# A decoder step on one core: selection and one-hot rows merged into one stream, expert rows fetched ahead, final norm without GpSimd

## The chip, the cores and the metric

The kernel runs on one core of a Trainium2 chip. The metric is the device time of one launch in microseconds (us): 2086.35 is the median of three runs (2083.2 to 2087.53). TensorE (PE in the profile) multiplies, VectorE (DVE) and ScalarE (ACT) do elementwise work, GpSimd (POOL) issues indirect transfers, SyncE (SP) issues most of the other transfers. Each engine works its own instructions in order; 16 DMA engines carry the transfers.

## What is computed

One layer of a decoder for 592 tokens (a prompt of 528 and eight samples of 8): two recurrent mixers, an output projection, then a product-key layer called PEER, then a norm. The change lies in PEER and the last norm:

```
def peer(xn, w_query, sub_keys, expert_u, expert_v):
    qh = einsum('td,de->te', xb, w_query).reshape(T, 8, 2, 128)
    s = einsum('thpd,hpnd->thpn', qh, sub_keys)            # 128 scores per half key
    sv, si = top_k(s, 16)
    cand = sv[:, :, 0, :, None] + sv[:, :, 1, None, :]     # 16 x 16 candidates
    top_s, pos = top_k(cand, 16);  eidx = expert numbers of the 16 winners, of 128*128
    gate = softmax(top_s)
    act = gelu(einsum('thkd,td->thk', expert_u[eidx], xb))
    return einsum('thk,thkd->td', gate * act, expert_v[eidx])
...
y = rms_norm(h, norm_final)
```

All arithmetic is float32. A product on PE is made of three, from a rounded high part and a rest (`mm3`: high by high, low by high, high by low).

## The kernel before

**Two ways for the experts.** 576 tokens reach PEER. For 416 of them (`ND`) the kernel computes every one of the 128 x 128 experts on PE: in `hidden` the pre-activations u·x of 128 experts at a time ("a half", 24 matmuls of 128 x 416 into the tile `pz`, two halves per step k), and in `experts` the sum over v (24 matmuls per half into eight accumulators `py`). The other 160 tokens (`NG`: 128 and 32, the 32 spread over four groups of partitions) take their expert rows one by one: `gather` fetches for each partition one row of u or v (128 x 1024, an indirect transfer that POOL issues into the ring `gr` of five buffers) and DVE multiplies it, 320 rows in all: 160 of u (line 1250, dot product) and 160 of v (line 1256, into `yt`).

**Each half's weights** come by SP seven halves ahead (`fetch`). ACT makes the high part (`uh`, line 1325, three halves ahead), DVE the low part (`ul`, line 1331, two halves ahead, three buffers). PE's third matmul of a half needs `ul`.

**Which experts count.** `scored` finds for each token the best 16 of each half key. Under `hidden`, a generator (`route`) does the rest in pieces, a few per half. `select` takes a block of 128 tokens: the candidates (`cand`), then for each of eight heads `top16`, five DVE instructions (max, index, replace, max, index; lines 987 to 992), each reading what the one before wrote; then a softmax numerator on ACT and a search of the indices (tiles `eq`, `sbx`). There are five blocks; block 0 belongs to the rows fetched one by one, blocks 1 to 4 give gates for the 416. `onehots` turns eight tokens' choices into one-hot tiles (three DVE instructions, lines 1171 to 1173; two buffers); 52 such sets. One half later `scatter` scales one of the tiles on ACT (eight instructions, line 1183), multiplies on PE (16 matmuls into `pw`, line 1193); later still ACT copies the result (`wst`, two instructions, line 1201), and SP stores it to DRAM for `experts` (1 MB for two sets). `hot(b-1)` runs the sets of a block one after the other, after `select(b)`.

**The order** of PE, DVE, ACT and SP from `hidden` on is the program's own (`in_order`). `fill(us)` decides what DVE gets in a half: it has a credit of `HALF - WL` = 3.35 us per half, takes a row of `gather` if a row is due (`gcred` grows by 1.1 per half, from the first half on), else the next piece of `route`, and pays the piece's nominal cost from the credit.

**Rows in runs.** 16 rows of u, then 16 rows of v for the 16 u of the run before. `gather` issues a row's transfer and, right behind it in the code, the DVE instruction that reads it.

**The end.** `gather_out` normalises the 160 tokens after the last row. Then the last pair of halves goes through PE accumulator by accumulator; DVE adds the residual (`yr`, line 1465), ACT squares, POOL sums six of the squares (line 185), PE sums over the partitions into one row of 416 (line 187), DVE copies it, PE turns it into a column per token (line 198), DVE and ACT take 1/sqrt, PE spreads it over the partitions (line 210), and DVE, ACT and POOL scale eight tiles `yo` that SP stores.

Of the kernel before, what the change touches and what calls it, by code (L numbers as in the profile page):

```python
# [40 lines left out]
PH = 8  # L41
# [5 lines left out]
XK = PH * TOPK // XG  # L47
NG = P + NX
# [15 lines left out]
GU, GV = 1.3, 1.3  # L64
GQ0, GQ1, GQ2, GTAIL = 1.1, 2.0, 1.7, 3
# [53 lines left out]
class Net:  # L119
# [69 lines left out]
    def rms_end(self, row, n, col, t, work):  # L189
# [6 lines left out]
        for b in range(nb):  # L196
            w = min(P, n - b * P)
            nc.tensor.matmul(col[:w, b:b + 1], rw[:, b * P:b * P + w], self.c("ones")[:1, :1], start=True, stop=True,
                             skip_group_check=True)
        r = work.tile([P, nb], F32, name="rmsr")  # L200
        nf = n // P
        if nf < nb:
            nc.vector.memset(r, 1.0)
            w = n - nf * P
# [3 lines left out]
        for b in range(nb):  # L208
            w = min(P, n - b * P)
            nc.tensor.matmul(t[:, b * P:b * P + w], r[:w, b:b + 1].to_broadcast([w, P]), self.c("ident")[:w, :w],  # L210
                             start=True, stop=True)
        return t[:, :n]
# [771 lines left out]
    def top16(self, src, n, sv, si, work):  # L984

        nc = self.nc
        nc.vector.max(sv[:n, 0:8], src)
        nc.vector.max_index(si[:n, 0:8], sv[:n, 0:8], src)
        t = work.tile([P, src.shape[-1]], F32, name="mr", tag=f"mr{src.shape[-1]}")
        nc.vector.match_replace(t[:n], sv[:n, 0:8], src, NEG)  # L990
        nc.vector.max(sv[:n, 8:16], t[:n])
        nc.vector.max_index(si[:n, 8:16], sv[:n, 8:16], t[:n])  # L992

    def scored(self):
# [21 lines left out]
        with self.pool("keys", 1) as kp, self.pool("qw", 2) as wp:  # L1016
            keys = kp.tile([P, 2 * PH, NK], F32, name="keys")
            nc.sync.dma_start(keys, I["keys"])
            for o, w in SEG:
                here = [(b, t0, n) for b, (t0, n) in enumerate(self.blks) if o <= t0 < o + w]  # L1020

                def scores(c, q):
# [4 lines left out]
                    for x, (b, t0, n) in enumerate(here):  # L1027
                        nc.scalar.activation(sc[:n, x, :], pc[:n, x, :], AF.Copy)
                        self.top16(sc[:n, x, :], n, sv[:, b, c // 2, c % 2, :], si[:, b, c // 2, c % 2, :], wp)
# [21 lines left out]
    def select(self, b):  # L1051
# [10 lines left out]
        yield 1.5  # L1062
# [23 lines left out]
        for x, rank in enumerate((a, r)):  # L1086
# [7 lines left out]
            yield 1.5  # L1094
            nc.vector.tensor_tensor(e[:n], e[:n], sx[:n], op=ALU.mult)
            yield 1.2
            w = TOPK
            while w > 1:
                w //= 2
                nc.vector.tensor_add(e[:n, :, :w, :], e[:n, :, :w, :], e[:n, :, w:2 * w, :])  # L1100
            v = small(f"ix{x}")
            nc.vector.tensor_copy(v[:n], e[:n, :, 0, :])
            out.append(v.rearrange("p h k -> p (h k)"))
            yield 1.8
# [52 lines left out]
    def onehots(self, q, last):  # L1157
# [12 lines left out]

        nc.vector.tensor_tensor(oh[0], io, rb(0), op=ALU.is_equal)
        nc.vector.tensor_tensor(oh[1], io, rb(1), op=ALU.is_equal)
        nc.vector.tensor_tensor(oh[2], oh[1], rb(2), op=ALU.mult)
        self.later(1, self.scatter, q, oh)
        yield 2.06

    def scatter(self, q, oh):
# [3 lines left out]
        for t in range(TG):  # L1181
            c = q * TG + t
            nc.scalar.activation(oh[3][:, t], oh[1][:, t], AF.Copy, scale=self.glo[:, c:c + 1])
# [21 lines left out]
    def route(self):  # L1205


        nblk = len(self.blks)

        def hot(b):  # L1210
            t0, n = self.blks[b]
            q0, q1 = t0 // TG, min(t0 + n, ND) // TG
            for q in range(q0, q1):
                yield from self.onehots(q, q == q1 - 1)

        yield from self.select(0)
        self.gready = True
        for b in range(1, nblk):
            yield from self.select(b)
            self.later(0, self.turned, b)  # L1220
            if b > 1:
                yield from hot(b - 1)
            else:
                yield 8.0
            yield from self.taken(b)
        yield from hot(nblk - 1)


    def gather(self):
# [3 lines left out]
        s = self.gstep  # L1233
        self.gstep += 1
        run, r = divmod(s, GL)
        runs = [(0, k) for k in range(4)] + [(1, k) for k in range(XK // GL)] + [(0, k) for k in range(4, PH * TOPK // GL)]

        seq = [("u", 0)] + [x for k in range(1, len(runs)) for x in (("u", k), ("v", k - 1))] + [("v", len(runs) - 1)]
        kind, k = seq[run]
        z, k = runs[k]  # L1240
        c = k * GL + r
        sl = slice(k * GL, (k + 1) * GL)
        gi, ga, xt, yt = self.gi[z], self.ga[z], self.xt[z], self.yt[z]
# [4 lines left out]
                                     in_offset=bass.IndirectOffsetOnAxis(ap=gi[:, x, c:c + 1], axis=0))  # L1248
# [7 lines left out]
        nc.vector.scalar_tensor_tensor(yt, t, ga[:, c:c + 1], yt, op0=ALU.mult, op1=ALU.add)  # L1256
        return GV

    def gather_out(self):
# [8 lines left out]
        for z, (y, n, o) in enumerate(((y0, P, NX), (y1[:NX], NX, 0))):  # L1268
            for t in part if z else ():
                nc.vector.tensor_add(y, y, t[:NX])  # L1270
            t = self.gp.tile([P, D], F32, name="gr", tag="gr")[:n]
            v = self.gp.tile([P, 1], F32, name="gv", tag="gv", bufs=1)[:n]
            nc.vector.scalar_tensor_tensor(t, y, 1.0, y, op0=ALU.mult, op1=ALU.mult, accum_out=v)
            nc.vector.tensor_scalar(v, v, 1.0 / D, EPS, op0=ALU.mult, op1=ALU.add)
            self.rsqrt(v, self.gp, bufs=1)
            nc.vector.scalar_tensor_tensor(t, y, v, self.gf[:n], op0=ALU.mult, op1=ALU.mult)
            nc.sync.dma_start(self.O["yg"][o:o + n], t)

# [9 lines left out]
    def run_due(self):  # L1288
# [3 lines left out]
        for _, f, a in sorted(now, key=lambda x: x[1] == self.scatter):  # L1292
            f(*a)

    def fill(self, us):

        self.credit += us
        while self.credit > 0:
            if self.gready and self.gcred >= 1 and self.gstep < 2 * (PH * TOPK + XK):
# [4 lines left out]
            if c is None:  # L1304
                self.routing = None
                self.credit = min(self.credit, 0.0)
                return
# [25 lines left out]
    def hidden(self):  # L1333
# [5 lines left out]
        self.gstep, self.gcred, self.gready = 0, 0.0, False  # L1339
# [7 lines left out]
        for k in range(NP):  # L1347
# [9 lines left out]
            for h in range(2):  # L1357
# [10 lines left out]
                self.gcred += GQ1 if kept else GQ0  # L1368
# [52 lines left out]
    def experts(self):  # L1421
# [4 lines left out]
        with self.pool("ew", 1) as wp, self.pool("ey", 1, space=PSUM) as yps:  # L1426
# [4 lines left out]
            rate = (2 * (PH * TOPK + XK) - self.gstep - KEEP * GQ2) / (2 * (NP - GTAIL) - KEEP)  # L1431
# [136 lines left out]
```

## Time and profile before

| | us |
|---|---|
| median of three runs | 2086.35 |
| the profiled execution | 2085.5 |
| its span, first to last instruction | 2083.7 |
| up to the first matmul of `hidden` | 805.0 |
| `hidden` | 674.8 |
| `experts`, to the last matmul | 574.2 |
| from there to the end | 29.7 |

PE is busy for 97% of the span, DVE for 76%, ACT for 44%, POOL for 28%; the DMA engines move 528 MB at a mean of 254 GB/s. A busy PE is not one at its peak: matmuls overlap, and their ends are modelled. The table's parts are cut at the first and last matmuls of `pz` and `py`.

### The profile page before, as it was taken

What the parts mean: (1) busy time and instruction counts of PE and PEld (TensorE: products, weight loads), DVE (VectorE), ACT (ScalarE), POOL (GpSimd) and SP (SyncE); (2) the same over time, 40 slices, a digit from 0 to 9 for tenths busy, and PEclk for the clock granted to TensorE, in tenths of its full rate; (3) what the DMA queues carried; (4) which work ended last, traced back from release to release, by engine and by line L of the source; (5) the groups of instructions that cost most, each with busy time, mean ns of one, the idle gap of its engine ahead of it and who ended that gap; (6) DMA issues with size and microseconds to landing.
All of it is one profiled execution on the core that took longest, in us unless ns stands there. A gap on an engine that the chain in (4) does not pass through costs nothing.

```text
span 2083.7 us, 34219 instructions
## 1 busy us (share of the span) xinstructions
PE 2020.4 (97%) x12752; PEld 1930.9 (93%) x12752; DVE 1587.6 (76%) x3026; ACT 925.5 (44%) x1654; POOL 585.0 (28%) x488
## 2 busy tenths in 40 slices
PE   7999999999999999899999999999999999999995
PEld 6998999798998898899999899899999999999994
DVE  6676665666465888798888798767988888888874
ACT  5532333253235444343676958953333333333331
POOL 1100000200003462522222131126654333343321
PEclk9999999999999999999999999999999999999997
DMA  7353333465556344888888898889999999999961
GB/s 250 111 170 105 96 98 97 152 180 175 175 165 210 102 140 155 316 316 296 282 323 287 293 321 288 307 322 372 385 388 390 385 372 370 367 364 369 361 242 46
DMA packets 242116, 528.23 MB, mean 254 GB/s; under 512 B 31269, under 2 KB 123173, under 8 KB 238493
## 3 DMA queue, kind: packets, MB, share of 16 engines
q1 hardware_dynamic: 195724, 358.24, 49.8%
q0 software_dynamic: 46080, 167.79, 22.6%
q8 instruction: 100, 1.64, 0.3%
q14 instruction: 68, 0.55, 0.1%
q10 hardware_dynamic: 144, 0.01, 0.0%
HBM read 448.55 MB, written 76.98 MB: 252 GB/s over the span
## 4 chain that ended last, share of the span: by engine, by line
PE 54%; DVE 3%; issue 1%; ACT 1%; DMA 1%; POOL 0%; DVEq 0%; ACTq 0%; POOLq 0%
PE py L135 9%; PE py L137 9%; PE py L136 9%; PE pz L135 8%; PE pz L137 8%; PE pz L136 8%; PE pw L1193 3%; DMA gr<-in_ur,gi 1%; DVE ul L1331 1%; ACT wst L1201 0%; ACT uh L1325 0%; POOL gr L1247 0%; POOL rmssum L185 0%; PE py L187 0%; DVE ti L992 0%
## 5 line engine op out<-in xcount | busy, mean ns | idle before, releaser
L1325 ACT ACTIVATE uh<-wr 128x1024 fp32r<-128x1024 f32 x256 | 271.1, 1059 | 370.4 <-PE py L136 183.9
L1331 DVE TENSOR_TENSOR ul<-wr,uh 128x1024 fp32r<-128x1024 f32 x256 | 312.3, 1220 | 85.6 <-issue 56.8
L137 PE MATMUL pz<-x2h,ul 128*128 128x416 f32 x1024 | 361.2, 353 | 10.3 <-DVE ul L1331 10.3
L135 PE MATMUL pz<-x2h,uh 128*128 128x416 f32 x1024 | 364.4, 356 | 0.0
L136 PE MATMUL pz<-x2l,uh 128*128 128x416 f32 x1024 | 360.5, 352 | 0.0
L135 PE MATMUL py<-ah,uh 128*128 128x416 f32 x1024 | 356.7, 348 | 0.6 <-ACT gk L1381 0.6
L137 PE MATMUL py<-ah,ul 128*128 128x416 f32 x1024 | 357.0, 349 | 0.0
L136 PE MATMUL py<-al,uh 128*128 128x416 f32 x1024 | 356.8, 348 | 0.0
L1247 POOL DMA_INDIRECT gr<-in_ur,gi x160 | 211.5, 1322 | 402.7 <-DVE gr L1250 208.9
L1247 POOL DMA_INDIRECT gr<-in_v,gi x160 | 213.0, 1331 | 379.3 <-DVE yt L1256 235.4
L135 PE MATMUL acc<-xnh,wh 128*128 128x296 f32 (+1 forms) x768 | 232.3, 303 | 7.6 <-ACT xnh L285 6.5
L136 PE MATMUL acc<-xnl,wh 128*128 128x296 f32 (+1 forms) x768 | 232.7, 303 | 0.5 <-DVE xnl L286 0.5
L137 PE MATMUL acc<-xnh,wl 128*128 128x296 f32 (+1 forms) x768 | 232.1, 303 | 0.3 <-DVE wl L131 0.3
L1256 DVE SCALAR_TENSOR_TENSOR yt<-gr,ga,yt 128x1024 f32<-128x1024 f32 x160 | 205.1, 1282 | 6.2 <-DMA gr<-in_v,gi 4.5
L137 PEld LDWEIGHTS pz<-x2h,ul 128*128 128x128 f32 x1024 | 194.0, 189 | 13.6 <-DVE ul L1331 12.7
L130 ACT ACTIVATE wh<-wr 128x1024 fp32r<-128x1024 f32 x104 | 110.0, 1058 | 208.3 <-issue 73.8
L1250 DVE SCALAR_TENSOR_TENSOR gr<-gr,xt 128x1024 f32<-128x1024 f32 x160 | 192.7, 1219 | 12.6 <-DMA gr<-in_ur,gi 12.5
L135 PEld LDWEIGHTS pz<-x2h,uh 128*128 128x128 f32 x1024 | 194.4, 190 | 3.4
L136 PEld LDWEIGHTS pz<-x2l,uh 128*128 128x128 f32 x1024 | 194.4, 190 | 0.9
L135 PEld LDWEIGHTS py<-ah,uh 128*128 128x128 f32 x1024 | 191.9, 187 | 1.0 <-ACT gk L1381 0.9
L136 PEld LDWEIGHTS py<-al,uh 128*128 128x128 f32 x1024 | 191.9, 187 | 0.3
L137 PEld LDWEIGHTS py<-ah,ul 128*128 128x128 f32 x1024 | 191.9, 187 | 0.0
(415 smaller groups left out, 3632.5 us busy)
## 6 DMA issues: line engine op xcount, KB each, us to landing
wr<-in_u SPq DMA_DIRECT2D x128, 512.0 KB, 6.0
wr<-in_v SPq DMA_DIRECT2D x128, 512.0 KB, 7.2
gz<-gz SPq DMA_DIRECT2D x112, 416.0 KB, 5.6
wd<-wst SPq DMA_DIRECT2D x26, 1024.0 KB, 7.4
wr<-in_w_in SPq DMA_DIRECT2D x48, 512.0 KB, 4.1
wj<-wd SPq DMA_DIRECT2D x96, 256.0 KB, 8.4
wr<-in_w_q SPq DMA_DIRECT2D x32, 512.0 KB, 3.7
wr<-in_w_out SPq DMA_DIRECT2D x16, 512.0 KB, 4.3
```

What stands on the lines that cost most here:

```text
L130: self.last_hi = self.nc.scalar.activation(hi, src, AF.Copy)
L135: mm(out, wh, xh, start=start, stop=False)
L136: mm(out, wh, xl, start=False, stop=False)
L137: self.last_mm = mm(out, wl, xh, start=False, stop=stop)
L1193: nc.tensor.matmul(pw[:, u, :], oh[0][:, t], oh[2 + x][:, t], start=x == 0, stop=x == 1)
L1247: nc.gpsimd.indirect_dma_start(out=t, out_offset=None, in_=src, in_offset=bass.IndirectOffsetOnAxis(ap=gi[:, x, c:c + 1], axis=0))
L1250: nc.vector.scalar_tensor_tensor(t, t, 1.0, xt, op0=ALU.mult, op1=ALU.mult, accum_out=ga[:, c:c + 1])
L1256: nc.vector.scalar_tensor_tensor(yt, t, ga[:, c:c + 1], yt, op0=ALU.mult, op1=ALU.add)
L1325: self.nc.scalar.activation(w, self.raws[s], AF.Copy)
L1331: self.nc.vector.tensor_sub(w, self.raws.pop(s), self.ws[s][0].bitcast(F32))
```

## The change

`top16` takes several rows at once and issues each of its five steps for all of them before the next step; `select` calls it for two heads at a time. `route` becomes two generators that take turns, one piece each: the selections of all five blocks in a row, and the one-hot sets of a block as soon as its selection is two halves old. The one-hot pieces are now single instructions, at most one set ends per half, and line 1172's instruction goes first. The eight scalings (`scaled`) stand ahead of the copies in a half. `gather` is cut in two: `gather_begin` issues the transfer of a row, `gather` reads the oldest one and begins another; four are begun right after `select(0)`, and `gcred` starts there, at -2.5, and grows by 1.25 per half. Rows of u and v alternate. The rows are to end six steps before the end instead of three, and `gather_out` runs in pieces in those halves. At the end DVE sums the squares, and PE takes the column per token from two of the tiles at once; four of the eight stores go through ACT's queue.

```diff
-    def top16(self, src, n, sv, si, work):
+    def top16(self, n, work, *rows):
...
+        for src, sv, si in rows:
+            v.max(sv[:n, 0:8], src)
+        for src, sv, si in rows:
+            v.max_index(si[:n, 0:8], sv[:n, 0:8], src)
...
-        for h in range(PH):
-            self.top16(cd[:n, h, :], n, tv[:, h, :], ti[:, h, :], wp)
-            yield 1.45
+        for h in range(0, PH, 2):
+            self.top16(n, wp, *((cd[:n, x, :], tv[:, x, :], ti[:, x, :]) for x in (h, h + 1)))
+            yield 2.4
...
-        yield from self.select(0)
-        self.gready = True
-        for b in range(1, nblk):
-            yield from self.select(b)
-            self.later(0, self.turned, b)
-            if b > 1:
-                yield from hot(b - 1)
...
+        def selects():
+            for b in range(nblk):
+                yield from self.select(b)
...
+                if b == 0:
+                    for _ in range(4):
+                        self.gather_begin()
+                    self.gready = True
+        def hots():
+            hot = -1
+            for b in range(1, nblk):
+                while b not in found or self.half < found[b] + 2:
+                    yield -1
...
+                for q in range(q0, q1):
+                    while hot == self.half:
+                        yield -1
+                    yield from self.onehots(q, q == q1 - 1)
+                    hot = self.half
...
+            if r == GL - 1:
...
+            self.gather_begin()
...
-            self.gather_out()
-            row, col, t = py[0][:1, :ND], py[1], py[2]
...
-                    self.rms_add(row, self.y[d - 2], d - 2, wp, 3)
+                if 1 < d:
+                    nc.vector.tensor_add(sq[0], sq[0], sq[d - 1])
+                nc.scalar.activation(sq[d], self.y[d], AF.Square)
...
+                for x in (0, KC - 1):
+                    nc.tensor.matmul(col[:w[b], b:b + 1], sq[x][:, b * P:b * P + w[b]], self.c("ones")[:, :1], start=x == 0, stop=x > 0)
...
-                nc.sync.dma_start(self.O["y"][:, k, :], o)
+                (nc.scalar if k % 2 else nc.sync).dma_start(self.O["y"][:, k, :], o)
```

Three places show what the code's order becomes. The first is DVE in the third half of `hidden`, before (two heads of the first selection, `tv` and `ti` being the winners and their places, and the low weights `ul`):

```order
L987 MAX tv<-cand 128x8
L988 MAX_INDEX ti<-tv,cand 128x8
L990 MATCH_REPLACE mr<-tv,cand 128x136
L991 MAX tv<-mr 128x8
L992 MAX_INDEX ti<-tv,mr 128x8
L987 MAX tv<-cand 128x8
L988 MAX_INDEX ti<-tv,cand 128x8
L990 MATCH_REPLACE mr<-tv,cand 128x136
L991 MAX tv<-mr 128x8
L992 MAX_INDEX ti<-tv,mr 128x8
L1331 TENSOR_TENSOR ul<-wr,uh 128x1024
```

and the same place on DVE in the changed kernel:

```order
L995 MAX tv<-cand 128x8 x2
L997 MAX_INDEX ti<-tv,cand 128x8 x2
L999 MATCH_REPLACE mr<-tv,cand 128x136 x2
L1001 MAX tv<-mr 128x8 x2
L1003 MAX_INDEX ti<-tv,mr 128x8 x2
L1384 TENSOR_TENSOR ul<-wr,uh 128x1024
```

The same ten instructions stand there, with the second head's between those of the first. The second place is ACT in the one-hot stretch, from one high weight part (`uh`) to the next, before (a half with two sets: copies `wst`, scaled tiles `oh`, spread indices `rep`, then the gelu `gz` of a half):

```order
L1325 ACTIVATE uh<-wr 128x1024
L1201 ACTIVATE wst<-pw 128x128x4 x4
L1183 ACTIVATE oh_12959<-oh_12957,glo 128x128 x8
L1183 ACTIVATE oh_12968<-oh_12966,glo 128x128 x8
L1155 ACTIVATE rep_13065<-ijg 128x192
L1364 ACTIVATE gz<-pz 128x416
```

and on ACT in the changed kernel, where 42 halves in a row read like this one:

```order
L1378 ACTIVATE uh<-wr 128x1024
L1194 ACTIVATE oh_13071<-oh_13069,glo 128x128 x8
L1217 ACTIVATE wst<-pw 128x128x4 x2
L1166 ACTIVATE rep_13140<-ijg 128x192
L1417 ACTIVATE gz<-pz 128x416
```

The second set of the half is gone to another half. Before, 16 halves hold two sets and 20 one. The third place is DVE at the end, the last adds of the residual and what follows them, before:

```order
L1465 TENSOR_TENSOR yr_16226<-yr_16226,py_16213 128x416
L1465 TENSOR_TENSOR yr_16227<-yr_16227,py_16214 128x416
L195 COPY rmsrw<-py_16215 1x416
L203 MEMSET rmsr 128x4
L205 TENSOR_SCALAR rmsr<-py_16216 32x1
```

and after:

```order
L1519 TENSOR_TENSOR yr_16250<-yr_16250,py_16237 128x416
L1521 TENSOR_TENSOR rmssum<-rmssum,rmssq 128x416
L1519 TENSOR_TENSOR yr_16251<-yr_16251,py_16238 128x416
L1521 TENSOR_TENSOR rmssum<-rmssum,rmssq 128x416
L210 MEMSET rmsr 128x4
L212 TENSOR_SCALAR rmsr<-py_16239 32x1
```

The sums that POOL had stand between the adds, and the copy of the row is gone.

## Rows read from the trace of the kernel before

**Rows 1.** Stretches: us, busy us of five engines, clock, DMA share, GB/s

```profile
805.00:1479.80 674.80, 659.52 (x3924) 630.04 (x3922) 565.96 (x1067) 406.67 (x866) 205.87 (x161) 0.98 0.85 306
1479.80:2040.00 560.20, 560.20 (x2999) 559.91 (x3000) 466.26 (x488) 184.22 (x194) 218.58 (x160) 1.00 0.98 357
...
2060.40:2083.70 23.30, 8.15 (x22) 3.97 (x22) 5.08 (x15) 1.78 (x4) 2.09 (x2) 0.50 0.20 73
```

**Rows 2.** Groups by line: count, busy, mean ns, idle before and releasers

```profile
L137 PE MATMUL pz<-x2h,ul 128*128 128x416 f32 x1024 | 361.2, 353 | 10.3 <-DVE ul L1331 10.3
...
L1250 DVE SCALAR_TENSOR_TENSOR gr<-gr,xt 128x1024 f32<-128x1024 f32 x160 | 192.7, 1219 | 12.6 <-DMA gr<-in_ur,gi 12.5
...
L1171 DVE TENSOR_TENSOR oh<-iob,rep 128x1024 f16<-128x1024 f16 x52 | 35.8, 689 | 46.1 <-PE pw L1193 43.2 <-ACT gz L1364 2.9
```

**Rows 3.** Timeline, DVE and PE, first rows: start, us, idle before

```profile
847.28 1.22 DVE L1058 TENSOR_TENSOR cand<-sv 128x1024 f32<-128x1024 f32 x1
...
853.51 1.29 DVE L1250 SCALAR_TENSOR_TENSOR gr<-gr,xt 128x1024 f32<-128x1024 f32 x1 [4.88 <-DMA gr<-in_ur,gi]
...
854.74 1.21 DVE L1331 TENSOR_TENSOR ul<-wr,uh 128x1024 fp32r<-128x1024 f32 x1
...
855.87 1.21 DVE L1250 SCALAR_TENSOR_TENSOR gr<-gr,xt 128x1024 f32<-128x1024 f32 x1
...
856.00 0.72 PE L137 MATMUL pz<-x2h,ul 128*128 128x416 f32 x1 [4.60 <-DVE ul L1331]
```

**Rows 4.** DVE timeline, the first selection

```profile
810.90 1.23 DVE L1058 TENSOR_TENSOR cand<-sv 128x1024 f32<-128x1024 f32 x1
...
812.29 0.30 DVE L987 MAX8 tv<-cand 128x8 f32<-128x136 f32 x1
...
813.92 0.28 DVE L987 MAX8 tv<-cand 128x8 f32<-128x136 f32 x1
...
835.16 1.23 DVE L1095 TENSOR_TENSOR eq<-eq,sbx 128x2048 bf16<-128x2048 bf16 x1 [2.62 <-ACT sbx L1091]
```

**Rows 5.** DVE timeline, last of `scored`, rows of several heads mixed

```profile
807.86 0.28 DVE L987 MAX8 sv<-sc 128x8 f32<-128x128 f32 x1
808.05 0.07 DVE L992 MATCH_VALUE_LOAD si<-sv,mr 128x8 f32 x1
808.32 0.07 DVE L988 MATCH_VALUE_LOAD si<-sv,sc 128x8 f32 x1
```

**Rows 6.** ACT timeline, two halves of the one-hot stretch

```profile
1276.52 0.52 ACT L1364 ACTIVATE gz<-pz 128x416 f32<-128x416 f32 x1 [0.43 <-PE pz L137]
...
1282.01 0.52 ACT L1364 ACTIVATE gz<-pz 128x416 f32<-128x416 f32 x1 [0.22 <-PE pz L137]
...
1284.33 4.78 ACT L1183 ACTIVATE oh<-oh,glo 128x128 f16<-128x128 f16 x16
...
1290.75 0.50 ACT L1364 ACTIVATE gz<-pz 128x416 f32<-128x416 f32 x1
```

**Rows 7.** Stretch of 20 us inside it, columns as in group 1

```profile
1280.00:1300.00 20.00, 19.33 (x142) 16.72 (x141) 13.31 (x18) 18.66 (x55) 1.87 (x2) 0.95 0.81 300
```

**Rows 8.** Timeline of the end, all engines

```profile
2053.00 4.05 DVE L1465 TENSOR_TENSOR yr<-yr,py 128x416 f32<-128x416 f32 x8
...
2053.60 0.35 PE L137 MATMUL py<-ah,ul 128*128 128x416 f32 x1
...
2054.73 5.62 POOL L185 TENSOR_TENSOR rmssum<-rmssum,rmssq 128x416 f32<-128x416 f32 x5 [46.43 <-ACT rmssq L182]
...
2067.06 0.15 DVE L205 TENSOR_SCALAR rmsr<-py 32x1 f32<-32x1 f32 x1 [1.71 <-PE py L198]
...
2068.57 2.21 PE L210 MATMUL py<-cst,rmsr 128*128 128x128 f32 x8 [1.55 <-DVE rmsr L161]
...
2071.37 3.44 DVE L1478 SCALAR_TENSOR_TENSOR yo<-yr,par,py 128x416 f32<-128x416 f32 x6 [2.85 <-ACT rb L1470]
```

**Rows 9.** Transfers of the last stretch: KB each, median us to landing

```profile
out_y<-yo SPq DMA_DIRECT2D x8, 208.0 KB, 2.4
```

More of the change, by code (lines that the diff above doesn't have):

```diff
@@ L47 @@
 XK = PH * TOPK // XG
+NROW = 2 * (PH * TOPK + XK)
 NG = P + NX
@@ L199, in rms_end, with rms_cols @@
                              skip_group_check=True)
+        return self.rms_cols(col, t, [min(P, n - b * P) for b in range(nb)], work)
+    def rms_cols(self, col, t, ws, work):
+        nc = self.nc
+        nb = len(ws)
         r = work.tile([P, nb], F32, name="rmsr")
-        nf = n // P
+        nf = sum(w == P for w in ws)
         if nf < nb:
             nc.vector.memset(r, 1.0)
-            w = n - nf * P
+            w = ws[nf]
             nc.vector.tensor_scalar(r[:w, nf:], col[:w, nf:], 1.0 / D, EPS, op0=ALU.mult, op1=ALU.add)
@@ L981, in ffn_sink @@
         return sink
-    def top16(self, src, n, sv, si, work):
[L986 to L992, printed above, removed]
+    def top16(self, n, work, *rows):
+        v = self.nc.vector
+        ts = [work.tile([P, src.shape[-1]], F32, name="mr", tag=f"mr{src.shape[-1]}") for src, _, _ in rows]
+        for src, sv, si in rows:
+            v.max(sv[:n, 0:8], src)
+        for src, sv, si in rows:
+            v.max_index(si[:n, 0:8], sv[:n, 0:8], src)
+        for t, (src, sv, si) in zip(ts, rows):
+            v.match_replace(t[:n], sv[:n, 0:8], src, NEG)
+        for t, (src, sv, si) in zip(ts, rows):
+            v.max(sv[:n, 8:16], t[:n])
+        for t, (src, sv, si) in zip(ts, rows):
+            v.max_index(si[:n, 8:16], sv[:n, 8:16], t[:n])
     def scored(self):
@@ L1226, in route @@
-        yield from hot(nblk - 1)
-    def gather(self):
+        found = {}
+        def selects():
+            for b in range(nblk):
+                yield from self.select(b)
+                if b:
+                    self.later(0, self.turned, b)
+                found[b] = self.half
+                if b == 0:
[7 more added lines that the diff above has]
+                    yield -1
+                yield from self.taken(b)
+                t0, n = self.blks[b]
+                q0, q1 = t0 // TG, min(t0 + n, ND) // TG
+                for q in range(q0, q1):
[3 more added lines that the diff above has]
+                    hot = self.half
@@ L1232, in gather, with gather_begin @@
+        b = hots()
+        for x in selects():
+            yield x
+            y = next(b)
+            if y > 0:
+                yield y
+        yield from b
+    def gather_begin(self):
         nc = self.nc
         s = self.gstep
+        if s == NROW:
+            return
         self.gstep += 1
-        run, r = divmod(s, GL)
         runs = [(0, k) for k in range(4)] + [(1, k) for k in range(XK // GL)] + [(0, k) for k in range(4, PH * TOPK // GL)]
-        seq = [("u", 0)] + [x for k in range(1, len(runs)) for x in (("u", k), ("v", k - 1))] + [("v", len(runs) - 1)]
@@ L1239, in gather @@
-        kind, k = seq[run]
+        if s < GL:
+            kind, k, r = "u", 0, s
+        elif s < 2 * len(runs) * GL - GL:
+            k, r = divmod((s - GL) // 2, GL)
+            kind, k = ("v", k) if s % 2 else ("u", k + 1)
+        else:
+            kind, k, r = "v", len(runs) - 1, s % GL
         z, k = runs[k]
         c = k * GL + r
-        sl = slice(k * GL, (k + 1) * GL)
-        gi, ga, xt, yt = self.gi[z], self.ga[z], self.xt[z], self.yt[z]
         t = self.gp.tile([P, D], F32, name="gr", tag="gr")
@@ L1291, in run_due @@
         self.due = [x for x in self.due if x[0] > self.half]
-        for _, f, a in sorted(now, key=lambda x: x[1] == self.scatter):
+        for _, f, a in sorted(now, key=lambda x: (x[1] == self.scatter) - (x[1] == self.scaled)):
             f(*a)
@@ L1298, in fill @@
         while self.credit > 0:
-            if self.gready and self.gcred >= 1 and self.gstep < 2 * (PH * TOPK + XK):
+            if self.gcred >= 1 and self.rows:
                 self.gcred -= 1
@@ L1306, in fill @@
                 self.credit = min(self.credit, 0.0)
+                return
+            if c < 0:
+                self.credit = min(self.credit, 1.0)
                 return
@@ L1448, in experts @@
                         self.fill(HALF - WL - MUL)
+                    if self.gready and self.gdone == NROW:
+                        self.gready, self.routing = False, self.gather_out()
                     self.lo(self.half + 2)
```

83 lines of the change are left out of this document (46 added, 37 removed).

## The prediction

> **What bounds the kernel now.** I read the busy shares by stretch first, then the groups by line, then the timelines of the engines that PE waits for. From half 0 of `hidden` to the last matmul PE is the bound: in `experts` it is busy without a gap, 2999 matmuls in 560.2 us, or 4.483 us for a half of 24 [rows 1]. The 128 halves of `hidden` would take 573.8 at that step, but take 674.8 [rows 1]. The 52 one-hot sets [rows 2] add their own matmuls: a half with one set runs from 1276.52 to 1282.01 by the gelu that follows each half, 5.49 us, so a set costs 1.0, and 52 of them 52. What is left, 49 us, is lost to waiting, in two places.
>
> The first is the one-hot stretch. A half with two sets takes 8.74 us (1282.01 to 1290.75) where PE has 4.48 + 2.0 = 6.48 of work: ACT scales 16 tiles in one go, 4.78 us, before the copies and the next half's weights [rows 6]. ACT is busy for 18.66 of 20 us in such a stretch, and the granted clock is 0.95 in it [rows 7]. DVE's next set also waits for PE to free a one-hot tile, 43.2 us in all [rows 2], but that is the same jam seen from DVE. There are 16 such halves in the order: 16 x 2.26 = 36 us.
>
> The second is the start, where DVE is late with the low weights: PE waits 10.3 us for them [rows 2], and the worst wait, 4.60, comes because DVE stood 4.88 us before the first fetched row, which needed 6.2 us from its indices to land [rows 3]. With the slow clock behind such waits, this place has the remaining 13.
>
> **The change, part by part, against the profiled execution (2085.5, span 2083.7).**
>
> *One set per half.* Nothing is taken from ACT's work, it is spread. A half with one set needs on ACT the 5.49 less the 0.22 it idled [rows 6], about 5.3 with two spread indices in it, a little over 5.0 with one. PE needs 5.49. So in the 42 halves in a row PE leads by 0.2 to 0.5 a half, and what hides ACT's set is PE's own half; were ACT 0.3 slower, each half would grow by that. DVE needs one low part (1.13, from 854.74 to 855.87 [rows 3]), three one-hot instructions (0.69 each [rows 2]) and 1.25 rows (1.23, from 853.51 to 854.74 [rows 3]): 4.7. Of the 36 us I leave 2 for spills and take 34 as gained.
>
> *Heads in pairs.* One after the other, a head's five instructions take 1.63 us (812.29 to 813.92) [rows 4]. No row shows pairs of heads, but the end of `scored` mixes independent ones: a max step is 0.19 and an index step 0.27 [rows 5]. Two max, two index and a replace taken like an index make 1.19. That would save 0.44 x 40 heads = 17.6 us of DVE; the bounds are 0 and 17.6, and I take the whole, since rows of the same instructions show it.
>
> The Trainium skill (VectorE: DVE Perf Modes, The DRAIN you can't avoid) speaks against this: it says that the pipe is flushed behind every DVE instruction, whether or not a semaphore stands between two, and that only fewer instructions help. By it the pairs would save nothing, which is the first rival below; rows 4 against rows 5 differ from it, with the same instructions 0.44 us per head apart.
>
> *Everything early.* The price of the merged stream is that DVE gets all five selections, 12 one-hot sets and 63 rows ahead of half 61, besides the low parts. Heads: 40 x 1.19 = 47.6. The rest of a selection: the first one lasts from 810.90 to 847.28, 36.4 us; less eight heads (13.0), seven low parts (7.9) and the wait of 2.62 it is 12.9 [rows 3, 4]; five make 64.5. Low parts: 59 x 1.13 = 66.7. Rows: 63 x 1.23 = 77.5, or 72.5 if a step is 1.15. One-hot: 36 x 0.69 = 24.8, or 22 if they overlap. Two hand-overs of gates: about 2. Together 275 to 283, begun at 810.90 as before, so DVE ends at 1086 to 1094. PE, from 805.0, reaches half 60 at 805 + 60 x 4.483 + 10 sets = 1084. **DVE and PE are level here,** DVE a little behind: 2 to 10 us. I take 6. This is the weak point of the change: in this stretch no DVE wait is covered any more.
>
> *Rows ahead of use.* POOL's transfers can start no sooner than before (five buffers, each freed by DVE), but DVE meets the first row only after three low parts and four pairs of heads, some 14 us after its issue against 6.2 to land [rows 3]. The wait of 4.88 and the burst of two to three rows a half behind it go. That is in the 6 us. Turning u and v about changes no count; a product with v needs its gelu two rows earlier, over a half, on an ACT with time to spare. Altogether the start loses 6 instead of 13; about 2 us at the first and last half stay.
>
> *`hidden` comes to* 573.8 + 52 + 2 + 6 + 2 = 636: 39 less than now. `experts` stays at PE's step: DVE is busy for 466 of 560 us there [rows 1], gets five rows fewer, and `gather_out` falls into halves without rows. It adds to SP's queue two stores that wait for DVE, with weights queued behind them; those are asked for seven halves ahead, 31 us. If that cover were too short, PE would wait; I put nothing on it.
>
> *The end.* PE's last matmul ends at 2053.95, and the mean of squares is taken at 2067.06, 13.1 later, behind POOL's five sums (5.62), PE's row, a copy and a turn [rows 8]. Now DVE's last add (4.05 / 8 = 0.51) and last sum follow the last matmul: 1.2 with the hand-over. The earlier sums lie between adds that wait for PE (6 x 0.187 = 1.12 per accumulator against 1.02). Then eight matmuls with a tile as weights. Four such cost eight records, 2.21 us, at a granted clock of 0.50 [rows 1, 8]: eight cost 4.4 at that clock and 2.2 at the full one. So 13.1 becomes 3.6 to 5.8; I take 5.8, 7.3 gained. Against it stands the last store: ACT's queue now holds the stores of tiles 1, 3 and 5 ahead of ACT's own tile 6, each waiting for DVE. DVE's fifth tile is ready 5 x 0.57 = 2.9 us after it begins; ACT's tile (0.5, as a gelu of that shape [rows 6]) and POOL's product (1.1, as a sum) follow: last issue at 4.5 instead of about 3.6, and 2.4 to land either way [rows 8, 9]. That takes 1 back. Net 6.3, between 5 and 8.5.
>
> *Sum:* 39 + 6.3 = 45, from 2085.5: 2040. The median lies 0.85 above the profiled execution: **2041.**
>
> **Rivals.**
>
> 1. *DVE bounds the first 60 halves.* If pairs save nothing, the level stretch grows by 17.6 us, and PE has no other work there: 2041 + 17 = 2058. For it: DVE has no slack there. Against it: the mixed rows [rows 4, 5]. 0.08.
>
> 2. *The DMA engines bound the one-hot run.* By the tiles' shapes a half in it moves 512 KB of weights, 208 of stored gelus, 512 of stored gates and 1.25 x 512 of rows: 1.92 MB in 5.49 us, 349 GB/s, for 230 us. `experts` moves 357 GB/s at a share of 0.98 without one gap on PE, and the present stretch 300 at 0.81 [rows 1, 7], so some 364 to 370 can be had, and it fits by 5%. If this mix of loads and stores allows only 330, a half takes 5.82, and 42 halves 14 us more: 2055. 0.10.
>
> 3. *The end gives nothing,* because the chain through ACT's queue and fp32 weights eats what POOL leaves: 2047. 0.05.
>
> 4. *Slower: the rows are met too early.* Halves 11 to 101 hold 116 rows, on a DVE without slack for half of the way. If each row is met before it lands and DVE waits, the low weights behind it are late and PE stands. From 0.39 us per row (45 / 116) the gain is gone; at 0.5 it costs 58: 2099. For it: the first row waited 4.88 [rows 3]. Against it: 160 rows of u waited 12.5 us in all [rows 2], and four rows ahead at 1.25 a half is 14 us. 0.05.
>
> **How the numbers follow.** The forecast, that PE sets the pace with single sets throughout, has 0.72, and spans 2032 to 2048 by the bounds above (DVE 2 to 10, spills 0 to 5, the end 5 to 8.5). To hold eight in ten and rival 2 and part of the wear between, I give 2031 to 2056. A measurement of this kernel tells about 0.2%, 4 us, from no change. Only rival 4 reaches that side: slower 0.04, within 0.2% 0.02, faster 0.94.
>
> **What would show it.** Right: no half of `hidden` over 6 us in the one-hot run, ACT just under PE there, granted clock at 1.00; the selection's max and index steps at 0.2 and 0.27; PE's waits for the low weights small and before half 60; no wait of DVE for a fetched row worth 2 us; the mean of squares 4 to 6 us after the last matmul; the last store about a microsecond later behind the scaling than now. Wrong: halves of 5.8 and more with DMA shares at 1.0 (rival 2), low weights late all through the first 60 halves (rival 1), or a long list of DVE waits for rows (rival 4).

## The result and the profile after

The changed kernel takes 2038.0 us, the median of four runs (2036.6 to 2039.6), against 2085.9 for the kernel before on the same chip: a ratio of 0.977, with an interval of 0.9755 to 0.9789. The forecast was 2041, in a range of 2031 to 2056. The profiled execution has a span of 2037.8, 45.9 less than before.

Where the 45.9 come from, cut at the same matmuls as the table ahead of the prediction:

| | before | after | forecast |
|---|---|---|---|
| up to the first matmul of `hidden` | 805.0 | 807.6 | 805 |
| `hidden` | 674.8 | 634.2 | 636 |
| `experts`, to the last matmul | 574.2 | 574.2 | 574 |
| last matmul to the mean of squares | 13.1 | 2.9 | 5.8 |
| from there to DVE's first scaled tile | 4.3 | 4.0 | |
| from there to the end | 12.4 | 14.8 | 13.3 |

The first row is no work of the change: the program up to there is the same. In the profiles of the experiments it takes 806.6 to 813.3 us, more where the granted clock of the first 200 us is lower (by 100 us: 0.98 and 0.95 after, 0.97 and 0.90 in the longest, 1.00 and 0.97 before). That alone sets these profiles up to 7 us apart. `experts` takes 574.2 in every one of the profiles, to a tenth, so below a part is judged by the stretch it lies in, and the ratio is given beside it.

Four stretches of the changed kernel: `hidden`, `experts`, DVE's first candidates to half 60, and halves 60 to 100 (columns: start:end, length, busy of PE, its weight loads, DVE, ACT, POOL, granted clock, DMA share, GB/s).

```profile
807.62:1441.80 634.18, 630.98 (x3923) 615.66 (x3921) 557.29 (x1070) 408.15 (x866) 240.13 (x166) 1.00 0.91 330
1441.80:2002.00 560.20, 560.18 (x2999) 559.87 (x3000) 468.23 (x506) 184.69 (x196) 204.51 (x155) 1.00 0.97 353
...
813.53:1094.80 281.27, 278.85 (x1603) 272.97 (x1602) 273.77 (x683) 157.93 (x268) 112.87 (x68) 1.00 0.84 297
...
1094.80:1318.90 224.10, 224.10 (x1644) 216.04 (x1642) 188.86 (x253) 205.27 (x534) 59.27 (x53) 1.00 0.95 354
```

Against [rows 1] DVE's work in `hidden` fell by 9 us (16 by the pairs, less six rows that now lie in it instead of in `experts`), ACT's rose by 1.5, and PE's granted clock is 1.00 where it was 0.98. In the last line 41 halves with one set each pass in 224.1 us, 5.47 each, and PE is busy for all of it. In the line above, DVE is busy for 273.8 of 281.3.

ACT in one half of that run, from one gelu (`gz`) to the next:

```profile
1203.46 0.52 ACT L1417 ACTIVATE gz<-pz 128x416 f32<-128x416 f32 x1 [0.47 <-PE pz L138]
1203.87 1.05 ACT L1378 ACTIVATE uh<-wr 128x1024 fp32r<-128x1024 f32 x1
1204.82 2.43 ACT L1194 ACTIVATE oh<-oh,glo 128x128 f16<-128x128 f16 x8
1207.16 1.06 ACT L1217 ACTIVATE wst<-pw 128x512 f32<-128x512 f32 x2
1208.12 0.35 ACT L1166 ACTIVATE rep<-ijg 128x192 f16<-128x192 f16 x1
1208.90 0.52 ACT L1417 ACTIVATE gz<-pz 128x416 f32<-128x416 f32 x1 [0.43 <-PE pz L138]
```

ACT works 5.0 us in this half, and waits 0.47 and 0.43 for PE ahead of the two gelus. It was the other way about in the halves of 8.74 us [rows 6]. Two groups by line, and DVE at its first selection:

```profile
L138 PE MATMUL pz<-x2h,ul 128*128 128x416 f32 x1024 | 358.8, 350 | 2.4 <-DVE ul L1384 2.4
...
L1295 DVE SCALAR_TENSOR_TENSOR gr<-gr,xt 128x1024 f32<-128x1024 f32 x160 | 194.7, 1218 | 0.1
...
814.92 0.51 DVE L995 MAX8 tv<-cand 128x8 f32<-128x136 f32 x2
...
817.36 1.20 DVE L1384 TENSOR_TENSOR ul<-wr,uh 128x1024 fp32r<-128x1024 f32 x1
```

PE waits 2.4 us for low weights, not 10.3, and DVE no longer waits for the u rows (0.1, not 12.6) [rows 2]. Two heads take 814.92 to 817.36: 1.22 us each, where one took 1.63 [rows 4].

The end, DVE, PE, ACT and POOL from the last add on:

```profile
2016.05 0.59 DVE L1519 TENSOR_TENSOR yr<-yr,py 128x416 f32<-128x416 f32 x1
2016.56 0.58 DVE L1521 TENSOR_TENSOR rmssum<-rmssum,rmssq 128x416 f32<-128x416 f32 x1
...
2018.95 0.15 DVE L212 TENSOR_SCALAR rmsr<-py 32x1 f32<-32x1 f32 x1 [1.79 <-PE py L1528]
...
2022.98 3.44 DVE L1539 SCALAR_TENSOR_TENSOR yo<-yr,par,py 128x416 f32<-128x416 f32 x6 [2.57 <-ACT rb L1531]
...
2024.61 0.64 ACT L1536 ACTIVATE yo<-yr,par 128x416 f32<-128x416 f32 x1 [1.66 <-DVE yo L1539]
...
2025.34 1.06 POOL L1537 TENSOR_TENSOR yo<-yo,rb 128x416 f32<-128x416 f32 x1 [84.86 <-ACT yo L1536]
2026.28 0.64 ACT L1536 ACTIVATE yo<-yr,par 128x416 f32<-128x416 f32 x1 [1.02 <-DVE yo L1539]
...
2027.00 1.06 POOL L1537 TENSOR_TENSOR yo<-yo,rb 128x416 f32<-128x416 f32 x1 [0.60 <-ACT yo L1536]
```

The last matmul ends at 2016.01. The mean of squares (line 212) follows 2.9 later. ACT's two tiles, which stood side by side before, now come 1.63 and 3.30 after DVE's first scaling, each behind a store in ACT's queue that waits for DVE, and POOL's second product ends at 2028.06.

### The profile page after: what moved, and what is told of

It reads as the page before. It is cut to its first block, busy times and chain, and to the rows that moved or that the text cites. A ratio compares the mean times of both kernels' runs of the same rounds, so it can differ in the third digit from the quotient of the medians.

```text
span 2037.8 us, 33976 instructions
## 1 busy us (share of the span) xinstructions
PE 1988.9 (98%) x12754; PEld 1917.1 (94%) x12754; DVE 1574.0 (77%) x3031; ACT 927.4 (46%) x1654; POOL 599.2 (29%) x483
## 4 chain that ended last, share of the span: by engine, by line
PE 57%; DVE 2%; issue 0%; ACT 0%; POOLq 0%; POOL 0%; DVEq 0%; ACTq 0%
PE py L136 9%; PE py L138 9%; PE py L137 9%; PE pz L136 9%; PE pz L138 9%; PE pz L137 9%; PE pw L1209 2%; DVE ul L1384 0%; DVE mr L999 0%; DVE ti L997 0%; DVE ti L1003 0%; DVE eq L1111 0%; DVE tv L995 0%; DVE eq L1106 0%; DVE tv L1001 0%
## 5 line engine op out<-in xcount | busy, mean ns | idle before, releaser
L1283 POOL DMA_INDIRECT gr<-in_ur,gi x160 | 225.7, 1411 | 370.6 <-DVE yt L1302 271.8
L1283 POOL DMA_INDIRECT gr<-in_v,gi x160 | 219.0, 1368 | 320.7 <-DVE gr L1295 255.1
```

Source lines behind the costliest of these rows:

```text
L1283: nc.gpsimd.indirect_dma_start(out=t, out_offset=None, in_=src, in_offset=bass.IndirectOffsetOnAxis(ap=self.gi[z][:, x, c:c + 1], axis=0))
```

## The experiments

All are the changed kernel with the edit shown. The changed kernel's own ratio is 0.9772.

| | ratio, interval | `hidden` | last matmul to mean | DVE's first scaled tile to end |
|---|---|---|---|---|
| changed kernel | 0.9772, 0.9755 to 0.9789 | 634.2 | 2.9 | 14.8 |
| e1 heads apart | 0.9820, 0.9804 to 0.9837 | 645.2 | 2.9 | 14.8 |
| e2 two sets | 0.9983, 0.9972 to 0.9994 | 677.8 | 3.0 | 14.8 |
| e3 two in even halves | 0.9861, 0.9844 to 0.9879 | 652.8 | 2.9 | 14.8 |
| e4 old norm | 0.9796, 0.9779 to 0.9812 | 634.3 | 4.3 | 14.8 |
| e5 other norm at the end | 0.9788, 0.9771 to 0.9805 | 634.2 | 9.4 | 14.8 |
| e6 stores on SP | 0.9755, 0.9738 to 0.9772 | 634.2 | 2.9 | 12.4 |
| e7 ACT's tiles first | 0.9764, 0.9749 to 0.9779 | 634.2 | 3.0 | 12.4 |
| e8 later fill | 0.9751, 0.9738 to 0.9765 | 631.6 | 2.9 | 14.8 |
| e9 both small edits | 0.9743, 0.9722 to 0.9765 | 631.8 | 2.9 | 12.4 |
| e10 rows at once | 0.9817, 0.9799 to 0.9835 | 646.1 | 2.9 | 14.8 |
| e11 rows in runs | 0.9772, 0.9753 to 0.9791 | 636.3 | 2.9 | 14.8 |
| e12 more traffic | 0.9803, 0.9783 to 0.9822 | 644.4 | 2.9 | 14.8 |

### Heads one after the other

```diff
-            self.top16(n, wp, *((cd[:n, x, :], tv[:, x, :], ti[:, x, :]) for x in (h, h + 1)))
+            for x in (h, h + 1):
+                self.top16(n, wp, (cd[:n, x, :], tv[:, x, :], ti[:, x, :]))
```

> The changed kernel with one edit: each head's five selection steps are issued one after the other again, in the same places of the program, so that nothing else moves. If pairing is what keeps DVE in step, a head costs 1.63 us again instead of 1.22, 40 heads 16 us more on DVE. In the trace of the changed kernel DVE is idle for about 7.5 of the 281 us from its first candidates to half 60, so 9 to 13 us reach PE as late low weights: 2047 to 2051. The first rival of the prediction (every DVE instruction is flushed whatever stands beside it, so the order of independent ones is worth nothing) gives no change: 2038. A third theory, that DVE is not what sets the pace there, gives under 3 us: 2038 to 2041.

`hidden` took 11.0 us more. DVE in the first selection, two heads' first steps; and who PE waited for in `hidden` (total, times, longest):

```profile
816.09 0.30 DVE L995 MAX8 tv<-cand 128x8 f32<-128x136 f32 x1
...
817.72 0.28 DVE L995 MAX8 tv<-cand 128x8 f32<-128x136 f32 x1
...
PE pz L138 <- DVE ul L1385: 8.2, 8, 2.8
```

A head is 1.63 again and PE waits 8.2 us for low weights instead of 2.4. These waits cost PE more than their own length: in the two halves that lose most, 4.4 and 4.5 us, the granted clock is 0.81. So pairing pays 16 us on DVE, 11 of which reach the end of `hidden`. This also shows that DVE is as short of time there as the prediction said.

It decides against the price of nothing that the prediction read from the Trainium skill (VectorE: DVE Perf Modes, The DRAIN you can't avoid), which has the pipe flushed behind every DVE instruction, with a semaphore or without: the order of the same instructions is worth 0.41 us a head here. The same section of the Trainium skill adds that a next instruction which is not held starts earlier, and the prediction left that out; whether this is what the pairs gain by, no run here shows.

### More than one set in a half

```diff
-            hot = -1
+            hot = []
...
-                    while hot == self.half:
+                    while hot.count(self.half) == 2:
                         yield -1
                     yield from self.onehots(q, q == q1 - 1)
-                    hot = self.half
+                    hot.append(self.half)
```

> The changed kernel with one edit: two one-hot sets may end in a half instead of one. The order then has 12 halves with two sets, most of them in runs (halves 71 to 73, 75 to 77, 82 to 84). The prediction's price, 2.26 us for every half with two sets, gives 27 us more: 2065. A rival read from the trace of before: the first double half of a run takes 6.49 us, no more than PE's own work, and only the ones behind it 8.5 to 9.7, because ACT has a store of high weights to draw on once. Five to seven halves would then cost 2.5 each, 12 to 17 us: 2050 to 2055. If ACT was not the cause of the long halves, no change: 2038.

The second kernel adds `or self.half % 2` to the condition.

> The changed kernel with one edit: sets may end in even halves alone, two at most. The order then has 10 halves with two sets, none next to another; ahead of each stands a half with one set, behind it a half with none. The prediction's price of 2.26 us for each double half gives 23 us more: 2061. The rival, that one double half alone is carried by ACT's lead and only runs of them cost, gives 0.2 to 0.5 each, 2 to 5 us: 2040 to 2043.

`hidden` took 43.6 us more in the first and 18.6 in the second. By ACT's scalings the first has 13 halves with two sets and the second 11, one more each than was expected, so a double half costs 3.4 and 1.7 us in the mean (singly, in the second, from nothing to 4.4). Neither the price of 2.26 nor the rival's 0.2 to 0.5 for single ones holds. PE's matmuls of the sets in two double stretches of the first kernel, and what it waited for in `hidden` of the first and of the second (total, times, longest):

```profile
1125.48 1.09 PE L1209 MATMUL pw<-oh,oh 128*128 128x128 f16 x16 [0.42 <-ACT wst L1217]
1130.38 0.66 PE L1209 MATMUL pw<-oh,oh 128*128 128x128 f16 x8 [3.81 <-ACT wst L1217]
1143.83 1.09 PE L1209 MATMUL pw<-oh,oh 128*128 128x128 f16 x16 [0.80 <-ACT wst L1217]
1148.73 1.01 PE L1209 MATMUL pw<-oh,oh 128*128 128x128 f16 x8 [3.81 <-ACT wst L1217]
...
PE pw L1209 <- ACT wst L1217: 26.4, 13, 3.8
...
PE pw L1209 <- ACT wst L1217: 13.7, 14, 2.6
```

PE waits for ACT's copies of the last products (`wst`), up to 3.81 us, since these now stand behind 8 or 16 scalings on ACT; in the kernel before they stood ahead of them. In the first kernel's double stretch, 1118 to 1290, the granted clock is 0.92 as well. What a double half costs thus depends on the order within ACT too, and the price of before does not carry over. No run puts the copies first again with one set per half, so what that order alone is worth stays open. ACT in one double half of the second kernel and the half behind it:

```profile
1118.05 0.52 ACT L1417 ACTIVATE gz<-pz 128x416 f32<-128x416 f32 x1 [0.18 <-PE pz L138]
1119.41 4.78 ACT L1194 ACTIVATE oh<-oh,glo 128x128 f16<-128x128 f16 x16
1125.05 0.51 ACT L1417 ACTIVATE gz<-pz 128x416 f32<-128x416 f32 x1
1132.25 0.52 ACT L1417 ACTIVATE gz<-pz 128x416 f32<-128x416 f32 x1 [3.33 <-PE pz L138]
```

The gelu of the double half starts without a wait, so it was ACT that came late to it. By the gelus the two halves take 14.2 us, where PE needs 11.9 for two halves and three sets. ACT cannot use the half with no scalings that follows: there it stands 3.33 us waiting for PE, which is behind. A double half is not paid back by an idle one. Of all the edits that undo a part, these two cost most: one set per half is the core of the change.

### The old norm, and the other norm at the end

The first kernel has the lines of the kernel before from the last adds to the mean of squares. The second puts the norm of the 160 tokens behind the last step again:

```diff
-                    if self.gready and self.gdone == NROW:
-                        self.gready, self.routing = False, self.gather_out()
...
-            assert self.routing is None
+            for _ in self.gather_out():
+                pass
```

> The changed kernel with the old way to the mean of squares at the end: GpSimd sums six squares, TensorE sums over the partitions into a row, DVE copies it, TensorE turns it. All else as changed, the stores on two queues too. In the changed kernel the mean of squares is taken 2.95 us after the last matmul instead of 13.1, so the old way should cost 10 us: 2048. By the prediction's own sum (13.1 to 5.8, the half clock) 7 us: 2045. If POOL's sums were hidden before the last matmul now that it has nothing else to do, 3 to 4 us: 2042.

> The changed kernel with one edit: the norm of the 160 tokens stands after the last step again, as before, in front of the last adds on DVE. The run with the old norm of the 416 took the mean of squares 4.3 us after the last matmul, so POOL's sums were not what made it 13.1 before. Theory now: it was the 11.4 us of this other norm on DVE (2041.63 to 2053.00 in the trace of before), behind which all eight adds had to queue. Here DVE would begin the adds about 1 us before the last matmul ends, and 8 adds and 6 sums of 0.51 follow: the mean at 9 to 9.5 instead of 2.95, 6 to 6.5 us more, 2044. By the prediction's account (POOL's sums, row and turn were the cost, the other norm's move worth nothing) no change: 2038.

With the old norm the ratio is 0.0024 higher (5 us, inside what the two intervals allow), but the end is only 1.4 us longer. POOL, DVE and PE there:

```profile
2015.51 5.76 POOL L186 TENSOR_TENSOR rmssum<-rmssum,rmssq 128x416 f32<-128x416 f32 x5 [70.07 <-ACT rmssq L183]
...
2021.02 0.59 DVE L1518 TENSOR_TENSOR yr<-yr,py 128x416 f32<-128x416 f32 x1 [0.54 <-PE py L138]
...
2025.27 0.15 DVE L212 TENSOR_SCALAR rmsr<-py 32x1 f32<-32x1 f32 x1 [1.05 <-PE py L199]
```

POOL's five sums take as long as before, but begin at 2015.51, while PE is still at its last accumulators (last matmul 2020.98): they are hidden but for the last 0.3 us. By the trace, all three theories of the first kernel were too high. With the other norm at the end it is 6.5 us:

```profile
2018.40 1.56 DVE L1518 TENSOR_TENSOR yr<-yr,py 128x416 f32<-128x416 f32 x3
...
2025.73 0.58 PE L1527 MATMUL py<-cst,rmssum 128*128 128x1 f32 x2 [6.38 <-DVE rmsr L210]
...
2028.79 0.15 DVE L212 TENSOR_SCALAR rmsr<-py 32x1 f32<-32x1 f32 x1 [3.10 <-PE py L1527]
```

The first three adds come back to back, as all eight did before [rows 8], since PE had their accumulators ready while DVE was at the other norm. In the kernel before, the last instruction of that norm ends right ahead of the adds too:

```profile
2051.79 1.27 DVE L1276 SCALAR_TENSOR_TENSOR gr<-yt,gv,gf 32x1024 f32<-32x1024 f32 x1
```

In the second kernel PE then stands 6.38 us for the sums, and its column matmuls take 3.06 us at a granted clock of 0.50 instead of 1.75 at 1.00. Read against the kernel before, each of the two kernels has one half of the change to the mean. The first has the earlier `gather_out` with the old norm, and its mean comes at 4.3 instead of 13.1: 8.8 gained. The second has the new norm with the late `gather_out`, at 9.4: 3.7 gained. Both together gain 10.2, since they overlap by 2.3: POOL's sums are exposed only behind a late DVE. So the place of `gather_out` was the larger cause of the late mean, and with it mended, taking GpSimd out of the norm adds 1.4.

### The last stores

```diff
-                (nc.scalar if k % 2 else nc.sync).dma_start(self.O["y"][:, k, :], o)
+                nc.sync.dma_start(self.O["y"][:, k, :], o)
```

> The changed kernel with one edit: all eight last stores go through SP's queue, as before, so that nothing on ACT's queue stands ahead of ACT's own tiles 2 and 6. The prediction put the two-queue order at a loss of 1 us; the traces show 2.5 (14.8 us from the first scaled tile to the end instead of 12.3). If the order on ACT's queue is the cause, the stretch is 12.3 again: 2.5 us less, 2035.5. If SP alone becomes the bound (eight issues took 3.88 us before), 0 to 1 less. If the two queues help, slower by up to 1.

```diff
-            for k in range(KC):
+            for k in (2, 6, 0, 1, 3, 4, 5, 7):
```

> The changed kernel with one edit: tiles 2 and 6, which ACT and POOL scale, come first in the code, the other six after them; the stores stay on two queues by the tile's number. If only ACT's late tiles cost, the stretch from the first scaled tile to the end falls from 14.8 to 12.3 or below: 2035 to 2035.5. If a second queue costs something of its own at the program's end, part of it stays: 1 us gained, 2037.

Both end 2.4 us sooner behind DVE's first scaled tile. Scaling in the first of them, all eight stores on SP:

```profile
2028.34 1.16 ACT L1536 ACTIVATE yo<-yr,par 128x416 f32<-128x416 f32 x2
2028.47 3.44 DVE L1539 SCALAR_TENSOR_TENSOR yo<-yr,par,py 128x416 f32<-128x416 f32 x6 [2.45 <-ACT rb L1531]
2029.05 2.08 POOL L1537 TENSOR_TENSOR yo<-yo,rb 128x416 f32<-128x416 f32 x2 [82.96 <-ACT yo L1536]
2029.15 3.88 SPq L1540 DMA_DIRECT2D out_y<-yo  x8
```

ACT's two tiles stand side by side again. In the second kernel they do so too, with the stores on two queues, and the gain is the same. So the second queue costs and gives nothing; what costs is that stores which wait for DVE stand ahead of ACT's own tiles.

### DVE's start, and both small edits

```diff
-        self.half, self.credit, self.due, self.sel, self.rep = 0, 0.0, [], {}, {}
+        self.half, self.credit, self.due, self.sel, self.rep = 0, -6.0, [], {}, {}
```

> The changed kernel with one edit: the account of DVE's time in the first halves starts at -6 us instead of 0, so that the first selection begins a half or two later and the low weights of halves 2 and 3 come first. In the changed kernel halves 2, 3, 8 and 10 lose 0.75, 1.5, 0.8 and 0.6 us. If DVE's lateness at the start is their cause, 2 to 3 us are gained: 2035 to 2036. If it only moves the same lateness to half 55 to 61, where selections then end, no change: 2038. If the selections end too late for the one-hot run, up to 3 us slower.

`hidden` is 2.6 us shorter. Who waited for whom in it (PE) and up to half 61 (DVE):

```profile
PE pz L138 <- DVE ul L1384: 0.2, 1, 0.2
...
DVE eq L1106 <- ACT sbx L1102: 9.0, 3, 5.7
DVE gr L1295 <- DMA gr<-in_ur,gi: 2.4, 1, 2.4
```

PE's waits for low weights are gone but for 0.2. The last sets end two halves later and cost nothing. DVE waits more, and it does not matter.

> The changed kernel with the two edits that gained in the traces: all last stores on SP's queue (the end 2.6 us shorter) and DVE's account starting at -6 us (`hidden` 2.6 shorter). They lie 1200 us apart and should add: 5.2 us less, 0.9747 of the kernel before, `hidden` 631.6 and 19.2 from the last matmul to the end. If either was chance of one profile, its stretch is back at 634.2 or 21.8.

Both stretches are as short together as apart, 2035.0 us in the median, 0.9743 of the kernel before. That is 5 us below the changed kernel by the traces (2.4 and 2.4); the intervals of the two ratios still overlap.

### Rows: all due at once, in runs, and more traffic beside them

```diff
-        self.gstep, self.gdone, self.gcred, self.gready, self.rows = 0, 0, -2 * GQ0, False, deque()
+        self.gstep, self.gdone, self.gcred, self.gready, self.rows = 0, 0, 0.0, False, deque()
...
-                self.gcred += (GQ1 if kept else GQ0) if self.gready else 0
+                self.gcred += GQ1 if kept else GQ0
```

> The changed kernel with one edit: rows fall due from the first half on, as before, instead of from -2.5 at the end of the first selection, so that some eleven are due at once when the first selection ends. By the prediction the wait for the first row (4.88 before) and the burst behind it come back: DVE stands about 4 us right behind the four begun transfers, PE gets its low weights that much late, and `hidden` takes 638 to 641 instead of 634.2: 2042 to 2045. Rival: DVE's slack of 7.5 us in the first 60 halves takes the wait, and rows done early leave more of it later: 634 to 635, 2038.

11.9 us more in `hidden`, above both. DVE and PE in it:

```profile
DVE gr L1295 <- DMA gr<-in_ur,gi: 12.4, 8, 4.1
...
PE pz L138 <- DVE ul L1384: 10.7, 8, 3.2
```

The first row waits 4.1 us, though its transfer was begun ahead, and seven more of the burst 8.3 together. Transfers begun ahead do not save DVE the wait where the reading follows right behind; the later start of the reading does. What the four transfers begun ahead give by themselves, no run shows.

> The changed kernel with one edit: rows of u and v come in runs of 16 again instead of in turn. The prediction gave the turn no price and no gain: `hidden` 634.2 within 1, 2038. Rival: a run of v rows (1.28 us each against 1.22) or a gelu due right ahead of its first v row makes DVE late in the first 60 halves, where it has 7.5 us of slack: 636 to 640 in `hidden`.

The rows were put back into the order of the kernel before by its own table of runs. The ratio is the changed kernel's; `hidden` is 2.1 us longer, with 1.1 of it in half 55. Turning u and v about is worth 2 us at most.

```diff
+        self.xl = self.dp.tile([41, P, D], F32, name="xl")
...
+                if 60 <= self.half < 101:
+                    x = self.half - 60
+                    nc.sync.dma_start(self.xl[x], I["ur"][x * P:(x + 1) * P])
```

> The changed kernel with 41 transfers of 512 KB more, one in each half from 60 to 100, from the table of u rows to a buffer in DRAM that nobody reads (nothing else is changed). It measures how much the DMA engines had left in the one-hot run, where 354 GB/s pass now at a share of 0.95. With 2.44 MB a half the engines must be full. By the prediction's ceiling of 364 to 370 GB/s a half would take 6.6 us; the weights are asked for 31 us ahead, and behind that 15 to 20 us reach PE: 2053 to 2058. If the ceiling is at 390, as single slices of before show, a half takes 6.26 and the lead covers all but 2: 2038 to 2042. If loads from and to DRAM count twice (1.92 + 1.0 MB), 7.5 us and more a half: 2080 and up.

`hidden` is 10.2 longer, between the first two cases. The stretch of it:

```profile
1100.00:1320.00 220.00, 218.30 (x1556) 206.05 (x1556) 175.10 (x237) 188.99 (x495) 53.64 (x49) 1.00 1.02 420
```

420 GB/s for 220 us, above the prediction's ceiling of 364 to 370 and above the 390 of the second theory; a copy within DRAM is counted once here. PE keeps its 5.47 us per half up to half 82. Behind that ACT waits 20.6 us in all for the stores of gates that free its tiles, and five of the halves up to 99 take 6.9 to 8.0 us. ACT also waits 10.0 for weights to land, but only from 1349 us on, behind the run, where PE loses nothing: the lead of seven halves held, and it was the stores of gates that reached PE. So the one-hot run of the changed kernel, at 354, is not at the bound.

## Why the prediction was right, point by point

**One set per half: right in kind, its price too high.** PE leads in all 41 halves of the run, at 5.47 us, and the run itself loses nothing (2 were allowed for spills). A set costs 0.98, forecast 1.0. That double halves cost time, e2 and e3 show; that each costs 2.26 whatever stands around it was wrong: 3.4 and 1.7 there. In the kernel before they cost 1.6 each. By the first matmul of each half in its trace, less 4.483 us for the half and 0.98 for a set, the 16 double halves take 6.49 to 9.73 us and lose 25 in all, the 20 single ones 6. So the jam was worth 31 us, not 36, and the first 44 halves lost 17 of the rest, not 13.

**`hidden`: 634.2, forecast 636, in part by two errors that cancel.** The run gave back 31 us where 34 were taken as gained; the first 44 halves, which lose 6.4 now, gave back 11 where some 5 were. Undoing the three parts one by one costs 11.0 (e1), 43.6 (e2) and 11.9 (e10), 66.5 in all, against 40.6 that `hidden` gained. So an undone part tells what it is worth in the changed kernel, not its share of the gain.

**Heads in pairs: right.** 1.22 per head, forecast 1.19, and undoing it costs 11 us, where the first rival's price was 17.

**DVE level with PE up to half 60: right.** DVE is busy for 97% of that stretch. Halves 1 to 59, from first matmul to first matmul, take 6.4 us more than 4.483 for a half and 0.98 for a set (4.8 before half 23, 1.6 behind it), forecast 6. The loss does not lie where I had it, "DVE a little behind" at the end of the stretch: 3.6 of it lie at the start, in halves 2, 3, 8 and 10, and e8 takes 2.6 back by starting later.

**Rows ahead of use: right in kind, too small in price.** I had the wait and the burst at 7 of 13 us; in the changed kernel, where DVE has no slack, putting both back costs 11.9 (eight waits of DVE, 12.4 us).

**The end: 8.0 gained, forecast 6.3, and the step is wrong in its reason.** I read POOL's sums (5.62) as the piece that made the mean late, and put nothing on moving `gather_out`. The first line of [rows 8], eight adds in 4.05 us without a gap, said that DVE was the late one. By e4 and e5 the move alone is worth 8.8 of the 13.1 and the norm without GpSimd alone 3.7. The sum came out near all the same because it took the last add to follow the last matmul, which holds only with the move. The bounds of 3.6 to 5.8 missed the 2.9 because the column matmuls were sized from the spreading ones, 2.2 us at the full clock and 4.4 at the half: all eight took 1.75, at a granted clock of 1.00.

**The last stores: right in kind, the term of 1 us measured 2.4.** I had only tile 6 behind stores; tile 2 stands behind one as well, and POOL's second product ends 5.1 behind the first scaling instead of 2.7.

**The rivals.** DVE as the bound by useless pairs fell with e1, the DMA engines as the bound with the run itself, 41 halves without a gap on PE, and with e12: the ceiling of 364 to 370, worked out from shares of busy time, was too low, since 420 passed. The end without gain fell with the trace. The slower case, rows met too early, has its mechanism in e10; in the changed kernel the rows wait 3.8 us in all, no place for it.

## What to carry to other kernels

Where one engine (here ACT) does a step's work in the time that the bound (here PE) needs for the step, spread the steps evenly: a double step costs more than the idle half behind it gives back. When an engine stands late in a chain, look first at what its own queue held just before, as the adds back to back showed here, and only then at the cost of the links behind it. In a queue that both computes and stores, put the engine's own computing ahead of stores that wait for another engine. And when two parts of a change meet in one wait, undo each of them before giving either a price: here 8.8 and 3.7 made 10.2.

## What the runs showed of the hardware

The span ends 9.7 us after POOL's last product in all fourteen profiles, as in before (2074.03 to 2083.7) and after (2028.06 to 2037.8), whether the stores use one queue or two. The 16 DMA engines moved 420 GB/s for 220 us in e12. The eight matmuls that take the column per token lasted 1.75 us at a granted clock of 1.00 in the changed kernel, where PE had stood for 1.18 us, and 3.06 at 0.50 in e5, where it had stood for 6.38.
